# Gate and up projection of a decoder layer: tokens as the stationary operand, 512 features moving, result transposed by VectorE blocks and DMA

## Chip, core and metric

One core of a Trainium2 chip runs the whole layer in one launch. The metric is the device time in microseconds (us), median of three runs. TensorE multiplies a stationary operand (128 x 128, loaded by a weight load of its own) with a moving operand of up to 512 columns and adds into PSUM banks of 128 x 512 fp32. VectorE (DVE), ScalarE (ACT) and GpSimd (POOL) do the elementwise work; SyncE (SP) issues the DMAs. Each engine works through its own queue in order.

## The reference, cut to what matters

One decoder layer on 256 tokens, model width 2048, in fp32. Attention comes first; the part that the change touches is the feed-forward block at the end, with 5632 hidden features:

```python
x = x + jnp.concatenate([o_mla, o_nsa], axis=-1) @ w_o[l]
h = rmsnorm(x, ffn_norm_g[l])
x = x + (jax.nn.silu(h @ w_gate[l]) * (h @ w_up[l])) @ w_down[l]
return rmsnorm(x, final_norm_g)
```

## The kernel before, in words

**Precision.** Every product is made of three: each fp32 operand is split into a high part `hi` (rounded to the fp32r format that TensorE takes) and the rest `lo`, and hi·hi, hi·lo and lo·hi are added in PSUM. For a weight tile ACT writes `whi` (the copy in L142) and DVE writes `wlo` (the subtraction in L144).

**The weight stream.** All weights pass as 354 tiles of 128 x 1024 (512 KB each; the first 16 are 880 wide) through one class, `Stream`. Tile n is loaded by a DMA on SP into one of three raw buffers (`wraw`, L118 to L121), split into one of three pairs (`whi`, `wlo`), and used by TensorE. A raw buffer comes free when the split of the tile three places earlier has been read out; a pair comes free when TensorE is done with the tile three places earlier. `get` (L150) records, in front of each use of tile n, the DMAs up to tile n+2 and the splits up to tile n+1.

**The order.** `program()` (L34) writes TensorE's order by hand. The queues of the other engines, SP's among them, are ordered by a scheduler from the recorded program; a DMA that waits on SP holds up every DMA behind it.

**The feed-forward block.** The normalised input, transposed, lies in `h2T` as 16 blocks of 128 model features by 256 tokens, high and low part side by side (512 columns); `transpose_x` (L650) writes it. The factor of the row norm (`rstd`) is put on later. For gate and up (`gate_up`, L789) the weights are stationary: a tile holds 8 blocks of 128 x 128 weights for one group of 128 hidden features. For each block, `whi` is loaded and 512 columns move (all of `h2T`, L798), then `wlo` is loaded and 256 columns move (the high part, L801). The result comes out as features x tokens, which is what `down` needs. `activate` (L822) adds the two halves of the bank (ACT and DVE), multiplies by the norm's factor, which was spread over the partitions by two TensorE transposes (`rb2`, L208), on POOL (L831), takes the silu on ACT, multiplies on DVE, and splits into `aT`. There are 44 feature groups, in two halves of 22; after each half comes `down` for that half (88 weight tiles in all), in which `aT` is stationary and the weights move, 512 columns at a time: per tile twelve matmuls of 512 columns (L863 to L865).

Gate and up are 176 weight tiles, numbers 90 to 177 and 222 to 309; down has 178 to 221 and 310 to 353. A tile of either kind has 6144 moving columns.

Of the kernel before, what the change touches and what calls it, by code (L numbers as in the profile page):

```python
# [16 lines left out]
P = 128  # L17
# [1 line left out]
D = 2048  # L19
KD = D // P  # L20
FF = 5632
NF = FF // P
NFH = NF // 2
EPS = 1e-6
NEG = -1e30
C_Q, C_KV, C_KR, C_NQ = 0, 512, 768, 832
# [7 lines left out]
def program():  # L34

    s = [("w", ("g1", k)) for k in range(KD)]

    def w(*keys):
        return [("w", k) for k in keys]

    def A(name, i):
        return [(name, i, 0), (name, i, 1)]

    s += [("rb0",)] + w(("q", 0, 0), ("q", 0, 1)) + [("gates",)] + w(("q", 1, 0)) + [("rope_k",)]
    s += w(("w1k", 0), ("q", 1, 1), ("w1k", 1), ("cq", 0, 0)) + [("ck",)] + w(("cq", 0, 1))
# [34 lines left out]
    for h in range(2):  # L80
        for f in range(h * NFH, (h + 1) * NFH):
            if f == 0:
                s += w(("gate", 0, 0), ("up", 0, 0)) + [("tp", 3)] + w(("gate", 1, 0), ("up", 1, 0))
                s += [("rb2",)] + w(("gate", 0, 1), ("up", 0, 1), ("gate", 1, 1), ("up", 1, 1))
            elif f > 1:
                s += w(*A("gate", f), *A("up", f))
        s += [("w", ("down", h, dg, j)) for dg in range(4) for j in range(NFH // 2)]
    return s


# [69 lines left out]
def layer_kernel(ctx: ExitStack, tc: tile.TileContext, a: dict, out: bass.AP):  # L160
# [489 lines left out]
    def transpose_x(dg):  # L650

        for k2 in range(2):
            tp = bank("S0" if k2 == 0 else "O", f"tp{dg}_{k2}")
            for kk in range(2):
                k = 4 * dg + 2 * k2 + kk
                for t in range(2):
                    nc.tensor.transpose(tp[:, kk * S + t * P:kk * S + (t + 1) * P], x[:, t, k * P:(k + 1) * P], ident)
            for kk in range(2):
                k = 4 * dg + 2 * k2 + kk
                g = gcols[:, 16 + k:17 + k]  # L660
                src = tp[:, kk * S:(kk + 1) * S]
                nc.scalar.activation(h2T[:, k, 0, :], src, AF.Copy, scale=g)
                nc.vector.scalar_tensor_tensor(h2T[:, k, 1, :], src, g, h2T[:, k, 0, :].bitcast(F32),
                                               op0=ALU.mult, op1=ALU.subtract)


    def w_in_block(key, w):
# [118 lines left out]
             "mpv": mla_pv, "tp": transpose_x}[op](*args)  # L786


    def gate_up(key, w):  # L789
        n, f, j = key  # L790
        hi, lo = w
        if j == 0:
            st[n, f] = bank("ds" if n == "gate" else "PT", f"{n}{f}")
        pt = st[n, f]
        for k2 in range(0, 8, 2):
            for kk in (k2, k2 + 1):
                k = 8 * j + kk
# [6 lines left out]
    while step[0] == "w":  # L804
        gate_up(step[1], W.get(step[1]))
        step = next(steps)
    transpose_x(*step[1:])
    nc.vector.tensor_reduce(ssq[:, 1, :, 0], ssq[:, 0, :, 0:4], axis=AX.X, op=ALU.add)
    rms_rstd(rstd[:, 3, :], ssq[:, 1, :, 0], D)
    att.close()  # L810

    fp = ctx.enter_context(tc.tile_pool(name="ffn", bufs=1))
    aT = fp.tile([P, NFH, 2, S], F32R, name="aT")
    gfin = fp.tile([P, D], F32, name="gfin")
    nc.gpsimd.dma_start(gfin, a["gfin"])
    W.apart = {len(order) - 2: fp, len(order) - 1: fp}

    def next_weights(*key):
        assert next(steps) == ("w", key)
        return W.get(key)  # L820

    def activate(h, f):  # L822

        t2 = fp.tile([P, 2, S], F32, tag="t2", name=f"t2_{h}_{f}", bufs=2)
        u = fp.tile([P, 2, S], F32, tag="gu", name=f"u_{h}_{f}", bufs=2)
        sl = fp.tile([P, S], F32, tag="sl", name=f"sl_{h}_{f}", bufs=2)
        for b, n in enumerate(("gate", "up")):
            pt = st[n, h * NFH + f]
            nc.scalar.copy(t2[:, b, :], pt[:, S:])
            nc.vector.tensor_add(t2[:, b, :], pt[:, 0:S], t2[:, b, :])  # L830
        nc.gpsimd.tensor_mul(u, t2, RB[:, None, :].to_broadcast([P, 2, S]))  # L831
        nc.scalar.activation(sl, u[:, 0, :], AF.Silu)
        nc.vector.tensor_mul(u[:, 1, :], sl, u[:, 1, :])
        split(aT[:, f, 0, :], aT[:, f, 1, :], u[:, 1, :])

    for h in range(2):
        done = 0
        while done < NFH:
            step = next(steps)
            if step[0] == "rb2":  # L840
                bcast_rows(RB, rstd[:, 3, :], bank2("ps_rb2")[:, 0, :])
                continue
            n, f, j = step[1]
            gate_up(step[1], W.get(step[1]))
            if (n, j) == ("up", 1):
                activate(h, f - h * NFH)
                done += 1
        for dg in range(4):
            if dg % 2 == 0:
                dn = bank2(f"dn{h}_{dg}")  # L850
                pts = [dn[:, 0, :], dn[:, 1, :]]
            else:
                pts = [bank("S0", f"dn{h}_{dg}_0"), bank("O", f"dn{h}_{dg}_1")]
            last = h == 1 and dg == 3
            ntile = NFH // 2

            def down(t, j, w, pt, first, end, c=slice(0, 512)):
                hi, lo = w
                for k in range(2):
                    f = 2 * j + k  # L860
                    wh, wl = (v[:, k * 512 + c.start:k * 512 + c.stop] for v in (hi, lo))
                    h_, l_ = aT[:, f, 0, t * P:(t + 1) * P], aT[:, f, 1, t * P:(t + 1) * P]
                    nc.tensor.matmul(pt, h_, wh, start=f == 2 * first, stop=False)  # L863
                    nc.tensor.matmul(pt, h_, wl, start=False, stop=False)  # L864
                    nc.tensor.matmul(pt, l_, wh, start=False, stop=f == 2 * end - 1)  # L865

            def add(t, c0, c1, pt, i):
# [69 lines left out]
def _pack(inp):  # L937
# [11 lines left out]
    for i, k in enumerate(order):  # L949
# [105 lines left out]
```

## Time and profile before

| | |
|---|---|
| Time, median of three runs (lowest, highest) | 1074.83 us (1074.31, 1075.9) |
| The profiled execution: its time, its span | 1075.57 us, 1073.8 us |
| TensorE busy | 1052.7 us, 98% of the span |
| VectorE, ScalarE, GpSimd busy | 652.9, 565.8, 207.5 us |
| Granted TensorE clock, mean | 0.994 of full speed |
| Weights: DMAs of 512 KB, DMA engines' share | 338, 53.6% |

The span counts from the first to the last instruction. A busy share of TensorE counts overlapping matmuls once, so it tells that the engine seldom waits, not how fast its columns pass; that is read from the starts of matmuls that follow each other. "L142" is line 142 of the kernel; `whi`, `wlo`, `wraw`, `aT`, `h2T` are the names of the buffers, `dn` is the result of `down`, `gate` and `up` those of the two projections.

### The profile page before, as it was taken

To read this page: it belongs to the slowest core of one execution; us is meant where nothing else is said; L and a number is where in the kernel's file an instruction comes from. 1 tells how busy PE (TensorE), PEld (TensorE's weight loads), DVE (VectorE), ACT (ScalarE), POOL (GpSimd) and SP (SyncE) were. 2 spreads that over 40 slices of the span, in tenths; PEclk is the share of its full clock that TensorE was granted. 3 is DMA by queue.
4 is the path that set the end of the run, shared out by engine and by line. 5 is a ranking of instruction groups with operands and counts; after the bars stand their busy time and mean duration, and the time that the engine had idled before them with its cause. 6 is when DMAs were issued, how large, how long until landed. Compare 5 with 4: busy or idle time off the path is not lost.

```text
span 1073.8 us, 16240 instructions
## 1 busy us (share of the span) xinstructions
PE 1052.7 (98%) x6126; PEld 923.7 (86%) x6126; DVE 652.9 (61%) x1004; ACT 565.8 (53%) x996; POOL 207.5 (19%) x209
## 2 busy tenths in 40 slices
PE   8999999899999999999999999999999999999997
PEld 8999999788888888888888888888888888888886
DVE  5678989875656555555555454455555555555554
ACT  5768888754455545545444333345454454444442
POOL 2244446433342101001010000001010010101110
PEclk9999999999999999999999999999999999999998
DMA  8854343334456555555555555555555555555553
GB/s 278 281 168 159 119 133 105 99 105 151 136 178 216 182 192 193 183 193 187 188 194 185 193 193 194 196 194 183 192 189 186 194 184 189 195 186 190 195 194 137
DMA packets 54831, 193.57 MB, mean 180 GB/s; under 512 B 6436, under 2 KB 7076, under 8 KB 54624
## 3 DMA queue, kind: packets, MB, share of 16 engines
q1 hardware_dynamic: 54288, 191.36, 53.6%
q0 software_dynamic: 464, 1.17, 0.3%
q8 instruction: 48, 0.79, 0.3%
q14 instruction: 31, 0.25, 0.1%
HBM read 190.41 MB, written 2.10 MB: 179 GB/s over the span
## 4 chain that ended last, share of the span: by engine, by line
PE 90%; DVE 3%; DMA 3%; ACT 1%; POOL 1%; issue 1%; SPq 0%; POOLq 0%; DVEq 0%; ACTq 0%
PE up L798 15%; PE gate L798 15%; PE gate L801 8%; PE up L801 8%; PE dn L863 7%; PE dn L864 7%; PE dn L865 7%; PE woM L743 1%; PE woM L744 1%; PE woM L745 1%; PE woN L745 1%; PE woN L743 1%; PE woN L744 1%; PE ps_q L213 1%; PE ps_q L214 1%; PE ps_q L215 1%
## 5 line engine op out<-in xcount | busy, mean ns | idle before, releaser
L144 DVE TENSOR_TENSOR wlo<-wraw,whi 128x1024 fp32r<-128x1024 f32 (+3 forms) x352 | 421.1, 1197 | 376.1 <-ACT whi L142 374.8
L142 ACT CAST whi<-wraw 128x1024 fp32r<-128x1024 f32 (+2 forms) x352 | 366.4, 1041 | 438.7 <-PE dn L865 126.7
L798 PE MATMUL gate<-h2T,whi 128*128 128x512 f32 x704 | 221.2, 396 | 0.0
L798 PE MATMUL up<-h2T,whi 128*128 128x512 f32 x704 | 221.1, 395 | 0.0
L831 POOL TENSOR_TENSOR u<-t,RB 128x512 f32<-128x512 f32 x44 | 57.1, 1298 | 554.0 <-DVE t L830 554.0
L801 PEld LDWEIGHTS up<-h2T,wlo 128*128 128x128 f32 x704 | 132.3, 188 | 31.3
L801 PEld LDWEIGHTS gate<-h2T,wlo 128*128 128x128 f32 x704 | 132.2, 188 | 31.2
L801 PE MATMUL gate<-h2T,wlo 128*128 128x256 f32 x704 | 138.3, 278 | 0.0
L801 PE MATMUL up<-h2T,wlo 128*128 128x256 f32 x704 | 138.3, 278 | 0.0
L863 PE MATMUL dn<-whi,aT 128*128 128x512 f32 x344 | 133.8, 389 | 0.0
L864 PE MATMUL dn<-wlo,aT 128*128 128x512 f32 x344 | 133.8, 389 | 0.0
L865 PE MATMUL dn<-whi,aT 128*128 128x512 f32 x344 | 133.8, 389 | 0.0
L146 POOL TENSOR_TENSOR wlo<-wraw,whi 128x256 fp32r<-128x256 f32 x70 | 88.7, 1267 | 127.0 <-ACT whi L142 113.4
L798 PEld LDWEIGHTS gate<-h2T,whi 128*128 128x128 f32 x704 | 107.3, 189 | 0.2
L798 PEld LDWEIGHTS up<-h2T,whi 128*128 128x128 f32 x704 | 107.2, 189 | 0.0
L865 PEld LDWEIGHTS dn<-whi,aT 128*128 128x128 f32 x344 | 64.6, 188 | 13.5
L863 PEld LDWEIGHTS dn<-whi,aT 128*128 128x128 f32 x344 | 64.6, 188 | 13.4
L864 PEld LDWEIGHTS dn<-wlo,aT 128*128 128x128 f32 x344 | 64.6, 188 | 13.1
L213 PE MATMUL ps_q<-hT,whi 128*128 128x256 f32 x128 | 37.5, 293 | 0.5 <-ACT RB L209 0.5
L214 PE MATMUL ps_q<-hT,whi 128*128 128x256 f32 x128 | 36.2, 283 | 0.0
L215 PE MATMUL ps_q<-hT,wlo 128*128 128x256 f32 x128 | 36.2, 283 | 0.0
L743 PE MATMUL woN<-whi,oT 128*128 128x512 f32 x64 | 26.6, 415 | 0.0
(335 smaller groups left out, 1517.7 us busy)
## 6 DMA issues: line engine op xcount, KB each, us to landing
wraw<-in_w_dram SPq DMA_DIRECT2D x338, 512.0 KB, 3.4
wraw<-in_g_dram SPq DMA_DIRECT2D x14, 440.0 KB, 5.3
x<-in_x_dram SPq DMA_DIRECT2D x4, 512.0 KB, 7.0
xt<-in_xT_dram SPq DMA_DIRECT2D x3, 512.0 KB, 6.0
out_dram<-x SPq DMA_DIRECT2D x5, 256.0 KB, 2.5
gfin<-in_gfin_dram POOLq DMA_DIRECT2D x1, 1024.0 KB, 6.0
out_dram<-x SPq DMA_DIRECT2D x2, 320.0 KB, 2.7
wraw<-in_g_dram SPq DMA_DIRECT2D x2, 256.0 KB, 4.2
```

What stands on the lines that cost most here:

```text
L142: nc.scalar.copy(hi[:, c0:c1], raw[:, c0:c1])
L144: nc.vector.tensor_sub(lo[:, c0:c2], raw[:, c0:c2], hi[:, c0:c2].bitcast(F32))
L146: nc.gpsimd.tensor_sub(lo[:, c2:c1], raw[:, c2:c1], hi[:, c2:c1].bitcast(F32))
L213: nc.tensor.matmul(ps, hi, act[:, 0, :], start=start, stop=False)
L214: nc.tensor.matmul(ps, hi, act[:, 1, :], start=False, stop=False)
L743: nc.tensor.matmul(pts[t], h_, wh, start=first, stop=False)
L798: nc.tensor.matmul(pt, hi[:, kk * P:(kk + 1) * P], h2T[:, k], start=k == 0, stop=False)
L801: nc.tensor.matmul(pt[:, 0:S], lo[:, kk * P:(kk + 1) * P], h2T[:, k, 0, :], start=False, stop=k == KD - 1)
L831: nc.gpsimd.tensor_mul(u, t2, RB[:, None, :].to_broadcast([P, 2, S]))
L863: nc.tensor.matmul(pt, h_, wh, start=f == 2 * first, stop=False)
L864: nc.tensor.matmul(pt, h_, wl, start=False, stop=False)
L865: nc.tensor.matmul(pt, l_, wh, start=False, stop=f == 2 * end - 1)
```

## The change

Gate and up take the form that `down` has. The 5632 features are cut in 11 blocks of 512, in three parts of 4, 4 and 3 blocks, each part followed by `down` for its features. A weight tile now holds 2 blocks of 128 model features by 512 hidden features. For each of these and each half of the tokens, three matmuls of 512 columns run with tokens stationary: hi·whi, hi·wlo, lo·whi. So the result comes out as tokens x features and has to be turned before `down`:

- `silu(b)`: ACT takes the silu from PSUM, with the norm's factor as a scale per partition (`r2`, brought into place by four small DMAs on SP in place of the two TensorE transposes).
- `act(b)`: for each half of the tokens DVE multiplies up, factor and silu out of PSUM and transposes 128 x 512 in blocks of 32 x 32 into `tr`. So that the halves interleave, `h2T` holds even tokens first, then odd ones.
- `move(b)`: 16 DMAs on SP, each from one group of 32 partitions to another (32 partitions x 4 runs of 64 fp32, 32 KB), put the 32 x 32 blocks in place in `ar`; ACT and DVE split `ar` into `aT`.

In TensorE's order `move(b)` stands behind the third tile of the next block's gate, or behind the second tile of `down` for the last block of a part. The copy in L142 and the subtraction in L144 are L144 and L146 of the changed kernel.

```diff
+PARTS = (0, 4), (4, 8), (8, 11)
...
+    for n, (b0, b1) in enumerate(PARTS):
+        moved = []
+        for b in range(b0, b1):
+            i = 2 if b == 0 else 3
+            s += w(*[("gate", b, j) for j in range(i)]) + ([("tp", 3)] if b == 0 else moved)
+            s += w(*[("gate", b, j) for j in range(i, 8)]) + [("silu", b)]
+            s += w(*[("up", b, j) for j in range(8)]) + [("act", b)]
+            moved = [("move", b)]
+        down = w(*[("down", n, dg, j) for dg in range(4) for j in range(2 * (b1 - b0))])
+        s += down[:2] + moved + down[2:]
...
-                src = tp[:, kk * S:(kk + 1) * S]
-                nc.scalar.activation(h2T[:, k, 0, :], src, AF.Copy, scale=g)
...
+                src = tp[:, kk * S:(kk + 1) * S].rearrange("p (c t) -> p t c", t=2)
+                hi, lo = (h2T[:, k, s, :].rearrange("p (t c) -> p t c", t=2) for s in range(2))
+                nc.scalar.activation(hi, src, AF.Copy, scale=g)
+                nc.vector.scalar_tensor_tensor(lo, src, g, hi.bitcast(F32), op0=ALU.mult, op1=ALU.subtract)
...
-                nc.tensor.matmul(pt, hi[:, kk * P:(kk + 1) * P], h2T[:, k], start=k == 0, stop=False)
...
-                nc.tensor.matmul(pt[:, 0:S], lo[:, kk * P:(kk + 1) * P], h2T[:, k, 0, :], start=False, stop=k == KD - 1)
+        for k in range(2):
+            kd = 2 * j + k
+            wh, wl = hi[:, k * 512:(k + 1) * 512], lo[:, k * 512:(k + 1) * 512]
+            for t, pt in enumerate(st[n, b]):
+                h_, l_ = h2T[:, kd, 0, t * P:(t + 1) * P], h2T[:, kd, 1, t * P:(t + 1) * P]
+                nc.tensor.matmul(pt, h_, wh, start=kd == 0, stop=False)
+                nc.tensor.matmul(pt, h_, wl, start=False, stop=False)
+                nc.tensor.matmul(pt, l_, wh, start=False, stop=kd == KD - 1)
...
+            nc.sync.dma_start(r2[64 * t:64 * t + 64, m:m + 1], rstd[m::2, 3, t:t + 1])
...
+    def silu(b):
+        for t in range(2):
+            sl = fp.tile([P, 512], F32, tag="sl", name=f"sl{b}_{t}", bufs=2)
+            nc.scalar.activation(sl, st["gate", b][t], AF.Silu, scale=r2[:, t:t + 1])
+            st["sl", b, t] = sl
+    def act(b):
+        tr = fp.tile([P, 16, 32, 2], F32, tag="tr", name=f"tr{b}")
+        for t in range(2):
+            av = fp.tile([P, 512], F32, tag="av", name=f"av{b}_{t}", bufs=2)
+            nc.vector.scalar_tensor_tensor(av, st["up", b][t], r2[:, t:t + 1], st["sl", b, t],
+                                           op0=ALU.mult, op1=ALU.mult)
+            nc.vector.transpose(tr[:, :, :, t], av)
+        st["tr", b] = tr
+    def move(b):
+        ar = fp.tile([P, 4, 4, 64], F32, tag="ar", name=f"ar{b}")
+        tr = st["tr", b].rearrange("p (jc jq) c t -> p jc jq (c t)", jq=4)
+        for i in range(4):
+            for jq in range(4):
+                nc.sync.dma_start(ar[32 * jq:32 * jq + 32, :, i, :], tr[32 * i:32 * i + 32, :, jq, :])
+        b0 = [b0 for b0, b1 in PARTS if b0 <= b < b1][0]
+        aT = fp.tile([P, 4, 2, S], F32R, tag=f"aT{b - b0}", name=f"aT{b}")
+        v = ar.rearrange("p j i c -> p j (i c)")
+        split(aT[:, :, 0, :], aT[:, :, 1, :], v)
+        st["aT", b] = aT
```

How the change moves instructions, at three places. First TensorE, in the middle of a gate tile; `gate_0` and `gate_1` of the changed kernel are the banks of the two token halves. Before:

```order
L798 MATMUL gate_4624<-h2T,whi_4586 128x512 x2
L801 MATMUL gate_4624<-h2T,wlo_4587 128x256 x2
L798 MATMUL gate_4624<-h2T,whi_4620 128x512 x2
L801 MATMUL gate_4624<-h2T,wlo_4621 128x256 x2
L798 MATMUL gate_4624<-h2T,whi_4620 128x512 x2
```

Now:

```order
L810 MATMUL gate_0_4519<-whi_4490,h2T 128x512
L811 MATMUL gate_0_4519<-wlo_4491,h2T 128x512
L812 MATMUL gate_0_4519<-whi_4490,h2T 128x512
L810 MATMUL gate_1_4520<-whi_4490,h2T 128x512
L811 MATMUL gate_1_4520<-wlo_4491,h2T 128x512
L812 MATMUL gate_1_4520<-whi_4490,h2T 128x512
```

Two matmuls of 512 and two of 256 columns with four weight loads became three of 512 with three.

Second SP, where the first block is moved; tiles 106 to 113 are the second block's gate, and `ar0` is the moved first block. Before, tiles 110 to 114 follow each other:

```order
L121 DMA wraw110_4663<-in_w_dram 128x1024
L121 DMA wraw111_4686<-in_w_dram 128x1024
L121 DMA wraw112_4720<-in_w_dram 128x1024
L121 DMA wraw113_4743<-in_w_dram 128x1024
L121 DMA wraw114_4765<-in_w_dram 128x1024
```

Now:

```order
L123 DMA wraw110_4551<-in_w_dram 128x1024
L123 DMA wraw111_4589<-in_w_dram 128x1024
L865 DMA ar0_4569<-tr0_4506 32x4x64 x16
L123 DMA wraw112_4607<-in_w_dram 128x1024
L123 DMA wraw113_4625<-in_w_dram 128x1024
```

The sixteen moves stand between the weight tiles that are the sixth and the seventh of the next block; so it is at all eleven moves.

Third DVE, at the end of the first block's up (tile 105) and in the tiles behind it:

```order
L146 TENSOR_TENSOR wlo107_4516<-wraw107_4488,whi107_4515 128x1024
L854 SCALAR_TENSOR_TENSOR av0_0_4507<-up0_0_4366,r2_4237,sl0_0_4356 128x512
L854 SCALAR_TENSOR_TENSOR av0_1_4510<-up0_1_4367,r2_4237,sl0_1_4358 128x512
L856 STREAM_TRANSPOSE tr0_4506<-av0_0_4507 128x512
L146 TENSOR_TENSOR wlo108_4536<-wraw108_4513,whi108_4535 128x1024
L856 STREAM_TRANSPOSE tr0_4506<-av0_1_4510 128x512
L146 TENSOR_TENSOR wlo109_4554<-wraw109_4533,whi109_4553 128x1024
L146 TENSOR_TENSOR wlo110_4592<-wraw110_4551,whi110_4591 128x1024
L146 TENSOR_TENSOR wlo111_4610<-wraw111_4589,whi111_4609 128x1024
L550 TENSOR_TENSOR aT0_4586<-ar0_4569,aT0_4586 128x4x256
L146 TENSOR_TENSOR wlo112_4628<-wraw112_4607,whi112_4627 128x1024
```

Before, DVE had at each feature group four operations of 128 x 256 between the `wlo` of four tiles; now four of 128 x 512 stand together at the end of a block, with one `wlo` among them, and the split of the moved block stands in front of the seventh tile's. ACT's queue has the copy into `aT0` at the same place, between `whi111` and `whi112`.

## Rows read from the trace of the kernel before

**Rows 1.** The page: busy time by engine, and the last chain's shares.

```profile
PE 1052.7 (98%) x6126; PEld 923.7 (86%) x6126; DVE 652.9 (61%) x1004; ACT 565.8 (53%) x996; POOL 207.5 (19%) x209
PE 90%; DVE 3%; DMA 3%; ACT 1%; POOL 1%; issue 1%; SPq 0%; POOLq 0%; DVEq 0%; ACTq 0%
```

**Rows 2.** Timeline of TensorE: start, length in us, engine, line, operation.

```profile
346.58 0.71 PE L798 MATMUL gate<-h2T,whi 128*128 128x512 f32 x2
...
399.62 0.63 PE L798 MATMUL up<-h2T,whi 128*128 128x512 f32 x2
400.08 0.40 PE L801 MATMUL up<-h2T,wlo 128*128 128x256 f32 x2
400.32 0.63 PE L798 MATMUL up<-h2T,whi 128*128 128x512 f32 x2
...
580.75 0.40 PE L863 MATMUL dn<-whi,aT 128*128 128x512 f32 x1
580.99 0.39 PE L864 MATMUL dn<-wlo,aT 128*128 128x512 f32 x1
```

**Rows 3.** Timeline of VectorE, where two results of down are added (22 tiles apart).

```profile
610.88 1.28 DVE L870 TENSOR_TENSOR x<-x,dn 128x512 f32<-128x512 f32 x2 [0.41 <-PE dn L865]
...
670.72 1.29 DVE L870 TENSOR_TENSOR x<-x,dn 128x512 f32<-128x512 f32 x2 [0.41 <-PE dn L865]
```

**Rows 4.** Timeline of all engines, one weight tile in down; idle before, and releaser.

```profile
599.80 0.39 PE L863 MATMUL dn<-whi,aT 128*128 128x512 f32 x1
600.00 1.05 ACT L142 CAST whi<-wraw 128x1024 fp32r<-128x1024 f32 x1 [1.67 <-PE dn L865]
...
601.09 1.23 DVE L144 TENSOR_TENSOR wlo<-wraw,whi 128x1024 fp32r<-128x1024 f32 x1 [1.50 <-ACT whi L142]
...
602.34 0.33 SPq L121 DMA_DIRECT2D wraw<-in_w_dram  x1
```

**Rows 5.** Weight buffers in 590 to 640 us: from issue to landing.

```profile
DMA to landing us min/median/max: 3.3/3.4/3.5
```

**Rows 6.** The page's DMA issues: queue, count, KB each, us from issue to landing.

```profile
out_dram<-x SPq DMA_DIRECT2D x5, 256.0 KB, 2.5
...
gcols<-in_gcols_dram SPq DMA_DIRECT2D x1, 19.0 KB, 1.8
```

**Rows 7.** Timeline of SP's queue at the start: DMAs issued one behind the other.

```profile
1.17 0.42 SPq L267 DMA_DIRECT2D xt<-in_xT_dram  x1
1.64 0.90 SPq L121 DMA_DIRECT2D wraw<-in_g_dram  x2
2.58 0.44 SPq L269 DMA_DIRECT2D xt<-in_xT_dram  x1
```

**Rows 8.** Issues of output DMAs (SP) and of one on POOL: nanoseconds, min/median/max.

```profile
L887 SPq DMA_DIRECT2D out_dram<-x x8: 332/400/458, 1063.1 to 1069.7; - x8
...
L815 POOL DMA_DIRECT2D gfin<-in_gfin_dram x1: 652/652/652, 337.3 to 337.3; - x1
```

**Rows 9.** VectorE's addition out of PSUM, 128 x 512: nanoseconds, min/median/max.

```profile
L870 DVE TENSOR_TENSOR x<-x,dn x15: 680/681/689, 610.9 to 1060.1; 128x512 f32<-128x512 f32 x15
```

**Rows 10.** Waits of TensorE: us in total, times, longest.

```profile
PE o L512 <- DVE pl L498: 2.6, 1, 2.6
PE ps_ropeq L590 <- DVE u_uq L595: 2.4, 1, 2.4
PE ps_hk L400 <- DVE hsk L395: 1.3, 1, 1.3
```

**Rows 11.** Stretches around these: us, busy PE PEld DVE ACT POOL, PEclk, DMA, GB/s.

```profile
189.00:192.00 3.00, 0.96 (x3) 0.87 (x4) 2.93 (x8) 3.00 (x9) 1.40 (x3) 0.83 0.56 175
192.00:195.00 3.00, 3.00 (x17) 2.82 (x16) 2.39 (x5) 2.52 (x8) 1.44 (x1) 0.60 0.08 14
213.00:216.00 3.00, 1.97 (x7) 1.41 (x8) 2.52 (x4) 1.24 (x2) 0.73 (x2) 0.82 0.01 3
216.00:219.00 3.00, 3.00 (x18) 3.00 (x18) 2.54 (x4) 0.00 (x0) 0.65 (x1) 0.61 0.46 172
```

More of the change, by code (lines that the diff above doesn't have):

```diff
@@ L21 @@
 FF = 5632
-NF = FF // P
-NFH = NF // 2
+PARTS = (0, 4), (4, 8), (8, 11)
 EPS = 1e-6
@@ L79, in program @@
         s += w(("woM", dg, 0), ("woM", dg, 1)) + [("tp", dg - 1)] + w(("woM", dg, 2), ("woM", dg, 3))
[L80 to L87, printed above, removed]
+    for n, (b0, b1) in enumerate(PARTS):
[8 more added lines that the diff above has]
+        s += down[:2] + moved + down[2:]
     return s
@@ L660, in transpose_x @@
                 g = gcols[:, 16 + k:17 + k]
-                src = tp[:, kk * S:(kk + 1) * S]
-                nc.scalar.activation(h2T[:, k, 0, :], src, AF.Copy, scale=g)
-                nc.vector.scalar_tensor_tensor(h2T[:, k, 1, :], src, g, h2T[:, k, 0, :].bitcast(F32),
-                                               op0=ALU.mult, op1=ALU.subtract)
+                src = tp[:, kk * S:(kk + 1) * S].rearrange("p (c t) -> p t c", t=2)
+                hi, lo = (h2T[:, k, s, :].rearrange("p (t c) -> p t c", t=2) for s in range(2))
+                nc.scalar.activation(hi, src, AF.Copy, scale=g)
+                nc.vector.scalar_tensor_tensor(lo, src, g, hi.bitcast(F32), op0=ALU.mult, op1=ALU.subtract)
     def w_in_block(key, w):
@@ L786, in layer_kernel, with pair @@
              "mpv": mla_pv, "tp": transpose_x}[op](*args)
+    def pair(n, name):
+        if n == "S1":
+            b = bank2(name)
+            return [b[:, 0, :], b[:, 1, :]]
+        return [bank(t, f"{name}_{i}") for i, t in enumerate(("S0", "O") if n == "S0" else (n, n))]
     def gate_up(key, w):
-        n, f, j = key
+        n, b, j = key
         hi, lo = w
         if j == 0:
[L793 to L797, printed above, removed]
-                nc.tensor.matmul(pt, hi[:, kk * P:(kk + 1) * P], h2T[:, k], start=k == 0, stop=False)
-            for kk in (k2, k2 + 1):
-                k = 8 * j + kk
-                nc.tensor.matmul(pt[:, 0:S], lo[:, kk * P:(kk + 1) * P], h2T[:, k, 0, :], start=False, stop=k == KD - 1)
-    W.share = 0
-    while step[0] == "w":
-        gate_up(step[1], W.get(step[1]))
+            i = b - [b0 for b0, b1 in PARTS if b0 <= b < b1][0]
+            st[n, b] = pair((("ds", "PT") if i % 2 == 0 else ("S0", "S1"))[n == "up"], f"{n}{b}")
+        for k in range(2):
[6 more added lines that the diff above has]
+                nc.tensor.matmul(pt, l_, wh, start=False, stop=kd == KD - 1)
+    W.share = 0
+    while True:
+        if step[0] == "w":
+            gate_up(step[1], W.get(step[1]))
+        else:
+            transpose_x(*step[1:])
+            break
         step = next(steps)
-    transpose_x(*step[1:])
     nc.vector.tensor_reduce(ssq[:, 1, :, 0], ssq[:, 0, :, 0:4], axis=AX.X, op=ALU.add)
     rms_rstd(rstd[:, 3, :], ssq[:, 1, :, 0], D)
+    r2 = cp.tile([P, 2], F32, name="r2")
+    for t in range(2):
+        for m in range(2):
+            nc.sync.dma_start(r2[64 * t:64 * t + 64, m:m + 1], rstd[m::2, 3, t:t + 1])
     att.close()
     fp = ctx.enter_context(tc.tile_pool(name="ffn", bufs=1))
-    aT = fp.tile([P, NFH, 2, S], F32R, name="aT")
     gfin = fp.tile([P, D], F32, name="gfin")
@@ L818, in next_weights @@
     def next_weights(*key):
[L819 to L834, printed above, removed]
@@ L836, in layer_kernel @@
-    for h in range(2):
+        while True:
+            step = next(steps)
+            if step[0] == "w":
+                assert step[1] == key
+                return W.get(key)
+            other(*step)
+    def silu(b):
[5 more added lines that the diff above has]
+        tr = fp.tile([P, 16, 32, 2], F32, tag="tr", name=f"tr{b}")
+        for t in range(2):
+            av = fp.tile([P, 512], F32, tag="av", name=f"av{b}_{t}", bufs=2)
[3 more added lines that the diff above has]
+        st["tr", b] = tr
@@ L837, in layer_kernel, with other @@
+    def other(op, *args):
+        {"silu": silu, "act": act, "move": move}[op](*args)
+    for h, (b0, b1) in enumerate(PARTS):
+        ntile = 2 * (b1 - b0)
         done = 0
-        while done < NFH:
+        while done < b1 - b0:
             step = next(steps)
[L840 to L847, printed above, removed]
@@ L848, in layer_kernel @@
-        for dg in range(4):
[L849 to L855, printed above, removed]
+            if step[0] == "w":
+                gate_up(step[1], W.get(step[1]))
+            else:
+                other(*step)
+                done += step[0] == "act"
+        last_part = h == len(PARTS) - 1
@@ L857, in down @@
+        kinds = ("ds", "PT", "S0", "S1") if (b1 - b0) % 2 == 0 else ("S0", "S1", "ds", "S0")
+        for dg in range(4):
+            pts = pair(kinds[dg], f"dn{h}_{dg}")
+            last = last_part and dg == 3
             def down(t, j, w, pt, first, end, c=slice(0, 512)):
@@ L861, in down @@
                     wh, wl = (v[:, k * 512 + c.start:k * 512 + c.stop] for v in (hi, lo))
-                    h_, l_ = aT[:, f, 0, t * P:(t + 1) * P], aT[:, f, 1, t * P:(t + 1) * P]
+                    aT = st["aT", b0 + f // 4]
+                    h_, l_ = aT[:, f % 4, 0, t * P:(t + 1) * P], aT[:, f % 4, 1, t * P:(t + 1) * P]
                     nc.tensor.matmul(pt, h_, wh, start=f == 2 * first, stop=False)
@@ L870, in add @@
                 nc.vector.tensor_add(xs, xs, pt)
-                if h == 1:
+                if last_part:
                     sq = fp.tile([P, 512], F32, tag="sq", name=f"fsq{t}{c0}", bufs=2)
@@ L905, in layer_kernel @@
                     add(t, cs, cs + 512, pts[t], dg)
-                    if h == 1:
+                    if last_part:
                         weigh(t, cs, cs + 512)
@@ L966, in _pack @@
         elif n in ("gate", "up"):
-            w[i] = _chunks(inp["w_" + n][0], 8 * k[2], 8 * k[2] + 8, k[1] * P, (k[1] + 1) * P)
+            w[i] = _chunks(inp["w_" + n][0], 2 * k[2], 2 * k[2] + 2, 512 * k[1], 512 * k[1] + 512)
         elif n == "down":
-            r = k[1] * NFH + 2 * k[3]
+            r = 4 * PARTS[k[1]][0] + 2 * k[3]
             w[i] = _chunks(inp["w_down"][0], r, r + 2, 512 * k[2], 512 * k[2] + 512)
```

## The prediction

> **What bounds the kernel now.** I read the page first: TensorE is busy 98% of the span and holds 90% of the chain that ended last [rows 1], so a change is worth what it does to the rate of TensorE's columns and what it lets TensorE wait. The rate comes from starts of matmuls in the timeline. In gate and up a pair of 512-column and a pair of 256-column matmuls take from 399.62 to 400.32, 0.70 us. Over the 84 tiles from 94 (346.58) to the first of down (580.75) that is 234.17 us, 2.788 a tile [rows 2]. In down two additions that are 22 tiles apart start 59.84 us apart, 2.720 a tile [rows 3]. Both kinds have 6144 columns, so gate and up lose 0.068 us a tile.
>
> The second thing to read is the weight chain, since the change puts 16 DMAs into the one queue that feeds it. Take the tile that TensorE begins at 599.80: the cast of the next but one starts 0.20 later (1.05), its subtraction at 601.09 (1.23), and when that has ended, SP issues at 602.34 the load into the buffer that came free, 2.54 us into the tile [rows 4]. The load lands 3.4 us after its issue [rows 5]. From issue to the first matmul on `wlo` it is 3.4 + 1.05 + 1.23 and some 0.2 between them, 5.9 us; the `whi` is there 1.3 sooner. I count from E, the end of a block's up. The tile behind the moves is the seventh of the next block: due at E + 16.32, its `wlo` two matmuls later, E + 16.55. So it must be issued by E + 10.65; without moves it would be at about E + 5.2. **SP's slack is 5.4 us.**
>
> **The change, part by part.**
>
> *The form of gate and up.* Three matmuls of 512 columns take the place of two of 512 and two of 256, exactly down's form, with the same columns in a tile. I take down's period for it: 176 x 0.068 = 11.9 us saved [rows 2, 3]. The two TensorE transposes for the norm's factor go: some 0.15 more. **-12.1.** The four small DMAs that replace them stand four tiles ahead of what they hold up, far from the first silu, and cost nothing.
>
> *The elementwise work.* The two silus a block stand on ACT and the adds, POOL's multiplications and the many small splits go: ACT and DVE were busy 53% and 61% [rows 1] and get less to do. At a block's end DVE has two products out of PSUM, two transposes, and one `wlo` among them. A product is priced by the addition out of PSUM of the same shape, 0.68 [rows 9]; it has one operand more, which I give nothing. No row shows a VectorE transpose: it lies between 0.3, half of the addition, and 1.23, the subtraction of twice its size [rows 4, 9]; I take half the latter, 0.62, as it is an operation between buffers like that one. The `wlo` of the tile before ends at E - 0.2, so: products to E + 1.2, a transpose to 1.8, `wlo` to 3.1, second transpose to 3.7. The delay of that `wlo` is under 2 us and the tile for it is due two tiles on: covered. The first move is issued at E + 3.75.
>
> For a 128x128 transpose of 16-bit values the Trainium skill (VectorE: DVE Perf Modes, The three transpose paths) states 311 ns; an estimate from that page, four times as much for four times the columns, is 1.24 us. By it the moves would begin 1.2 us later and the sum would be some 13.6 us higher. No run here shows it yet.
>
> *The moves.* Sixteen to a block, on SP, each 32 KB in 128 runs of 256 B. Each issue holds SP for a spacing m, and behind them waits the load of the seventh tile, with all later loads, then the cast on ACT, the subtraction on DVE, and TensorE. That load is issued at E + 3.75 + 16m and used from E + 9.65 + 16m; due is E + 16.55. **The stall is 16m - 6.9 us a block, none below m = 0.43.** So m decides all. Bounds: a weight load is 0.33 [rows 4], with the 0.05 between two issues 0.38. Loads issued one behind the other at the start are spaced 0.47 (1.17 to 1.64; the next 0.94 for two) [rows 7], output issues are 0.33 to 0.46 [rows 8]. All of these are loads and stores whose descriptors the built program carries ready-made; the moves, like the one DMA issued on POOL, are not of that kind there. POOL's took 652 ns to issue [rows 8], with the gap 0.70. It is another engine and another queue, so it is a bound and not a price. I take the middle of 0.47 and 0.70, **m = 0.58**: a stall of 2.4 us, at ten blocks **24 us**. Some of the later moves also wait for the landing of the eighth before; with eight spacings (4.6 us) against landings of 1.8 to 2.5 [rows 6] that adds nothing.
>
> *The last move.* In parts one and two, of four blocks each, the older three feed down's first six tiles, so the block just finished is needed at the seventh, E + 16.32, which the stall above already covers. In part three, of three blocks, it is needed at down's fifth tile, E + 10.88. There the last move is issued at 3.75 + 15m, lands about 2.0 later [rows 6], and is cast in 1.05 [rows 4], with some 0.8 until the low part follows: the stall is 15m - 3.3, **5.4 us**.
>
> *The clock.* Waits of TensorE of 2.6 and 2.4 us [rows 10] were followed by granted clocks of 0.83 and 0.60, and 0.82 and 0.61, in two stretches of 3 us [rows 11]: 3 x (0.17 + 0.40) = 1.7 us lost each, part of it at the lower of the two levels, 1.2 of 2.4 GHz. My stall of 2.4 is as long, but it is cut in two by one matmul between the wait for `whi` and that for `wlo`. The wait of 1.3 us [rows 10] has no such stretch of its own in the rows. I take the loss for half of ten blocks and for the last: 5 x 1.7 + 1.7 = **10.2**; both ends, 1.7 and 18.7, stay in the range.
>
> *Sum.* -12.1 + 24 + 5.4 + 10.2 = +27.5 on the profiled 1075.57 is 1103.1; the profiled execution lies 0.7 above the median, so **1102 us**.
>
> **The rivals.**
>
> *Faster: issues as short as any on SP in this trace.* With m from 0.38 to 0.46 the load behind the moves is in time or 0.5 us late; what remains is the last block (2.4 to 3.6), one loss of clock and up to 5 us of stalls: -12.1 + 4.1 to -12.1 + 10.5, **1067 to 1073**. For it: every SP issue of before [rows 4, 7, 8]. Against it: none of them is of the moves' kind. The Trainium skill has a sentence for this side (DMA: Bandwidth & Descriptors, Issuing engines are not separate DMA queues): issue time on an engine "is usually small relative to the DMA itself". In this trace 0.33 stands against a landing of 3.4, which agrees for a load of 512 KB; sixteen of 32 KB the rows don't show. Chance 0.18.
>
> *Same: hold and gain cancel.* With m from 0.46 to 0.49 the stalls take 5 to 9 us, the last block 3.6 to 4.1 and one or two losses of clock 2 to 3: 1073 to 1077. Chance 0.10.
>
> *Slower still: the transposes or the moves are late too.* With transposes of 1.23 and m = 0.58, the first move is 1.2 later, the stall 3.6 at ten blocks and 6.6 at the last; with the clock of more blocks lost: about **1118**; with m = 0.70 at the short transposes, 43 + 7.2 + 18.7 - 12.1 = +57, **1132**. Part of slower.
>
> *The form doesn't give down's rate.* Gate and up would stay at 2.788, 12 us above every case: 1114 at my m, and slower even at m = 0.43. Against it: the same sequence of matmuls runs at 2.720 in down for 88 tiles, with the same buffers. Chance 0.03.
>
> **How the numbers follow.** 0.2% (2.1 us) is about what a measurement of this kernel can tell from no change. The forecast, stalls at ten blocks (m over 0.49, the later rivals with it), has 0.72: slower. Same 0.10, faster 0.18. Faster's own low end with m = 0.38 is 1067, the high end with m = 0.70 is 1132; beyond them I leave about 0.1 above (late transposes and slow issues together) and 0.05 below. Since faster and same hold 0.28, the range reaches to them. The slower case's own range is 1080 to 1132.
>
> **What would show it.** In the trace of the changed kernel: the matmul starts in the middle of gate, 2.72 a tile (else the form's term is wrong); SP's issues of `ar<-tr` and their spacing, which is m; the transpose's duration; the waits of TensorE on the cast and the subtraction of the seventh tile of each block, ten times 16m - 6.9, and none in other tiles; a longer wait on `aT` at the last part's fifth tile; the granted clock behind each. I am wrong on the sign if m is 0.46 or less, or if the loads behind the moves turn out to land much faster or slower than 3.4 us, since the moves' short runs share the DMA engines with them.

## The result, and the profile after

The changed kernel took 1137.66 us (median; 1134.05 to 1138.46) against 1075.01 for the kernel before: a ratio of 1.0576, 95% interval 1.0551 to 1.0600. Slower by 62.65 us, where 1102 was predicted; above the range's upper end of 1132. The profiled execution took 1134.05 us, the lowest of the four, with a span of 1132.3 against 1073.8.

The page of the changed kernel, the lines that answer to [rows 1]: busy time, and the shares of the last chain. SP's queue, which had none of the chain, now has 10%, most of it on the line of the moves (L865).

```profile
PE 1071.2 (95%) x5420; PEld 906.4 (80%) x5420; DVE 633.9 (56%) x891; ACT 535.3 (47%) x852; POOL 148.9 (13%) x165
PE 71%; SPq 10%; DVE 8%; DMA 5%; ACT 3%; issue 3%; POOL 0%; POOLq 0%; DVEq 0%; ACTq 0%
SPq L865 9%; PE up L812 7%; PE up L810 7%; PE up L811 7%; PE dn L899 5%; PE dn L900 5%; PE dn L898 5%; DMA wraw<-in_w_dram 4%; PE gate L811 4%; PE gate L812 4%; PE gate L810 3%; DVE wlo L146 3%; ACT whi L144 2%; PE woM L745 1%; PE woM L746 1%
```

The waits of TensorE from gate to the end (total us, times, longest). In the kernel before this stretch had none.

```profile
PE gate L810 <- ACT whi L144: 23.4, 8, 3.3
PE dn L898 <- ACT whi L144: 5.7, 2, 3.0
PE gate L811 <- DVE wlo L146: 5.5, 8, 0.8
PE dn L898 <- ACT aT L549: 5.2, 1, 5.2
PE dn L899 <- DVE wlo L146: 1.1, 3, 0.5
```

Eight blocks wait in the next gate and two in down, for the cast and then for the subtraction of the tile behind the moves; the eleventh waits for its own `aT`. That is the place and the number of times that were forecast. The new operations: nanoseconds, min/median/max, of the products, the transposes and the moves' issues.

```profile
L854 DVE SCALAR_TENSOR_TENSOR av<-up,r,sl x22: 740/744/751, 377.2 to 1050.9; 128x512 f32<-128x512 f32 x22
L856 DVE STREAM_TRANSPOSE tr<-av x22: 698/703/707, 378.5 to 1053.3; 128x512 f32<-128x512 f32 x22
L865 SPq DMA_DIRECT2D ar<-tr x176: 593/599/1275, 381.0 to 1063.6; - x176
```

One stall, in the timeline of all engines but TensorE: the end of the second block (E is 427.27).

```profile
427.09 3.87 SPq L123 DMA_DIRECT2D wraw<-in_w_dram  x2
...
430.52 0.70 DVE L856 STREAM_TRANSPOSE tr<-av 128x512 f32<-128x512 f32 x1
431.25 10.27 SPq L865 DMA_DIRECT2D ar<-tr  x16
...
436.71 1.23 DVE L146 TENSOR_TENSOR wlo<-wraw,whi 128x1024 fp32r<-128x1024 f32 x1 [1.50 <-ACT whi L144]
441.62 9.26 SPq L123 DMA_DIRECT2D wraw<-in_w_dram  x6
442.95 1.05 ACT L549 CAST aT<-ar 128x1024 fp32r<-128x1024 f32 x1 [6.27 <-DMA ar<-tr]
444.03 1.23 DVE L550 TENSOR_TENSOR aT<-ar,aT 128x1024 fp32r<-128x1024 f32 x1 [6.09 <-ACT aT L549]
445.69 1.04 ACT L144 CAST whi<-wraw 128x1024 fp32r<-128x1024 f32 x1 [1.69 <-DMA wraw<-in_w_dram]
446.77 3.76 DVE L146 TENSOR_TENSOR wlo<-wraw,whi 128x1024 fp32r<-128x1024 f32 x3 [1.51 <-ACT whi L144]
```

The moves hold SP from 431.25 to the next load's issue at 441.62, 10.37 us or 0.648 for each of sixteen. ACT waits for that load until 445.69. On TensorE:

```profile
443.36 0.39 PE L812 MATMUL gate<-whi,h2T 128*128 128x512 f32 x1
446.79 0.79 PE L810 MATMUL gate<-whi,h2T 128*128 128x512 f32 x1 [3.04 <-ACT whi L144]
448.05 0.79 PE L811 MATMUL gate<-wlo,h2T 128*128 128x512 f32 x1 [0.47 <-DVE wlo L146]
448.64 0.63 PE L812 MATMUL gate<-whi,h2T 128*128 128x512 f32 x1
449.07 0.63 PE L810 MATMUL gate<-whi,h2T 128*128 128x512 f32 x1
...
455.81 0.39 PE L810 MATMUL up<-whi,h2T 128*128 128x512 f32 x1
...
461.25 0.39 PE L810 MATMUL up<-whi,h2T 128*128 128x512 f32 x1
```

From start to start, 443.36 to 448.05 is 4.69 us for two matmuls that else take 0.45: a stall of 4.2. Behind it a matmul takes 0.43 instead of 0.227 for some four us. The last two rows are two tiles apart, 5.44 us: 2.72 a tile, the rate of down. In stretches of that stall (us, busy PE, PEld, DVE, ACT, POOL, then the granted clock, the DMA engines' share, GB/s):

```profile
443.00:447.00 4.00, 0.96 (x5) 0.50 (x3) 1.46 (x2) 2.08 (x3) 0.00 (x0) 0.92 0.97 345
447.00:451.50 4.50, 4.03 (x9) 2.85 (x10) 3.44 (x3) 2.05 (x2) 0.00 (x0) 0.50 0.65 173
451.50:455.50 4.00, 4.00 (x15) 3.18 (x15) 1.23 (x1) 1.21 (x2) 0.00 (x0) 0.78 0.61 236
```

**The ledger.** From gate's first matmul to down's last it was 731.4 us before and is 791.4 now, 60.0 more. I summed every interval between the starts of neighbouring matmuls there, less the usual 0.227, wherever it was over 0.3. Intervals with a wait in them come to 41.0 us at the ten blocks (3.8 to 4.5 each) and 5.8 at the last (5.4 of it the wait for `aT`); intervals without one, in the time behind a stall, to 24.1 us (1.4 to 3.0 at each of eleven, 2.2 on average); small ones elsewhere to 0.5. 60.0 - 41.0 - 5.8 - 24.1 - 0.5 = -11.4 is the form's gain.

### The profile page after: what moved, and what is told of

It is laid out like the page before. It is cut to its first block, busy times and chain, and to the rows that moved or that the text cites. A ratio compares the mean times of both kernels' runs of the same rounds, so it can differ in the third digit from the quotient of the medians.

```text
span 1132.3 us, 14758 instructions
## 1 busy us (share of the span) xinstructions
PE 1071.2 (95%) x5420; PEld 906.4 (80%) x5420; DVE 633.9 (56%) x891; ACT 535.3 (47%) x852; POOL 148.9 (13%) x165
## 4 chain that ended last, share of the span: by engine, by line
PE 71%; SPq 10%; DVE 8%; DMA 5%; ACT 3%; issue 3%; POOL 0%; POOLq 0%; DVEq 0%; ACTq 0%
SPq L865 9%; PE up L812 7%; PE up L810 7%; PE up L811 7%; PE dn L899 5%; PE dn L900 5%; PE dn L898 5%; DMA wraw<-in_w_dram 4%; PE gate L811 4%; PE gate L812 4%; PE gate L810 3%; DVE wlo L146 3%; ACT whi L144 2%; PE woM L745 1%; PE woM L746 1%
## 5 line engine op out<-in xcount | busy, mean ns | idle before, releaser
L146 DVE TENSOR_TENSOR wlo<-wraw,whi 128x1024 fp32r<-128x1024 f32 (+3 forms) x352 | 416.2, 1183 | 385.1 <-ACT whi L144 382.8
L144 ACT CAST whi<-wraw 128x1024 fp32r<-128x1024 f32 (+2 forms) x352 | 366.4, 1041 | 459.3 <-PE up L812 140.0
L810 PE MATMUL gate<-whi,h2T 128*128 128x512 f32 x352 | 144.2, 410 | 23.4 <-ACT whi L144 23.4
L811 PE MATMUL gate<-wlo,h2T 128*128 128x512 f32 x352 | 145.2, 412 | 5.5 <-DVE wlo L146 5.5
L898 PE MATMUL dn<-whi,aT 128*128 128x512 f32 x344 | 137.2, 399 | 10.9 <-ACT whi L144 5.7
L812 PE MATMUL gate<-whi,h2T 128*128 128x512 f32 x352 | 143.6, 408 | 0.0
L810 PE MATMUL up<-whi,h2T 128*128 128x512 f32 x352 | 136.9, 389 | 0.0
L811 PE MATMUL up<-wlo,h2T 128*128 128x512 f32 x352 | 136.9, 389 | 0.0
L812 PE MATMUL up<-whi,h2T 128*128 128x512 f32 x352 | 136.9, 389 | 0.0
L900 PE MATMUL dn<-whi,aT 128*128 128x512 f32 x344 | 136.5, 397 | 0.0
L926 POOL TENSOR_TENSOR x<-x,gfin 128x512 f32<-128x512 f32 (+1 forms) x7 | 9.7, 1405 | 768.5 <-ACT fsq L908 768.5
L810 PEld LDWEIGHTS gate<-whi,h2T 128*128 128x128 f32 x352 | 70.4, 200 | 41.8 <-ACT whi L144 26.7
L811 PEld LDWEIGHTS gate<-wlo,h2T 128*128 128x128 f32 x352 | 70.1, 199 | 23.3 <-DVE wlo L146 8.4
L812 PEld LDWEIGHTS gate<-whi,h2T 128*128 128x128 f32 x352 | 70.3, 200 | 14.9
L812 PEld LDWEIGHTS up<-whi,h2T 128*128 128x128 f32 x352 | 66.1, 188 | 13.8
L811 PEld LDWEIGHTS up<-wlo,h2T 128*128 128x128 f32 x352 | 66.1, 188 | 13.7
L810 PEld LDWEIGHTS up<-whi,h2T 128*128 128x128 f32 x352 | 66.1, 188 | 13.6
```

What stands on the lines that cost most here:

```text
L144: nc.scalar.copy(hi[:, c0:c1], raw[:, c0:c1])
L146: nc.vector.tensor_sub(lo[:, c0:c2], raw[:, c0:c2], hi[:, c0:c2].bitcast(F32))
L810: nc.tensor.matmul(pt, h_, wh, start=kd == 0, stop=False)
L812: nc.tensor.matmul(pt, l_, wh, start=False, stop=kd == KD - 1)
```

## The experiments

The theory: the moves' issues hold SP's in-order queue for longer than the weight stream's slack, and each stall is followed by matmuls at the low clock (0.50 in the rows above). Rival A: the moves' short runs take the DMA engines from the weights. Rival B: DVE is late at a block's end. Each run has the changed kernel as its base, unless it names another.

### The moves spread among the weight loads

```diff
-        s += down[:2] + moved + down[2:]
+                for q in range(4):
+                    s += [("move", b - 1, q)] + gate[3 + q:4 + q]
...
-        for i in range(4):
-            for jq in range(4):
-                nc.sync.dma_start(ar[32 * jq:32 * jq + 32, :, i, :], tr[32 * i:32 * i + 32, :, jq, :])
+        for jq in range(4):
+            nc.sync.dma_start(ar[32 * jq:32 * jq + 32, :, q, :], tr[32 * q:32 * q + 32, :, jq, :])
```

> The sixteen moves of each of the first ten blocks stay on SP, but stand in three groups (8, 4 and 4) with one weight load between each two; those of the last block stay together. Theory (each move holds SP's queue for 0.64 us, and sixteen in a row are more than the 6.8 us from the first move to the time at which the next load is due): eight hold it for 5.2 us from E + 3.9 to E + 9.1, before the E + 10.65 at which the load behind them is due, four for 2.6. No stall at ten blocks, no low clock behind them; the stall of the last block (5.3 us, and 2.4 of low clock) stays. 1075 - 12.3 + 7.7 = 1070 us, 1069 to 1073. Rival A (the moves' short runs share the DMA engines with the weights and make those land late): the same bytes move, 1115 or more. Rival B (DVE is late at a block's end): nothing of it is changed, 1125 or more.

Measured: 1081.32 us, ratio 1.0048 (1.0033 to 1.0063). The same 176 moves on the same queue, and 56 us less. SP's queue at the first block, and TensorE's waits from gate on:

```profile
379.72 0.33 SPq L134 DMA_DIRECT2D wraw<-in_w_dram  x1
380.40 5.27 SPq L877 DMA_DIRECT2D ar<-tr  x8
385.78 0.53 SPq L134 DMA_DIRECT2D wraw<-in_w_dram  x1
386.35 2.53 SPq L877 DMA_DIRECT2D ar<-tr  x4
```

```profile
PE dn L912 <- ACT aT L560: 7.5, 3, 5.2
PE dn L914 <- DVE aT L561: 1.3, 2, 0.6
PE up L822 <- DVE wlo L157: 0.8, 2, 0.5
PE dn L913 <- DVE wlo L157: 0.6, 1, 0.6
```

No wait for a `whi` is left. Rivals A and B, which kept all their causes here, are out as the main cause. The 11 us above my 1070 are a miss of its own: three waits on `aT`, not one. At the ends of parts one and two the spread moves (12 and 4 there) bring the newest block later than the seventh tile of down wants it; with the low clock behind them the three cost 14.6 us by the ledger's way of counting (4.1, 2.4, 8.2).

### No moves

```diff
-        ar = fp.tile([P, 4, 4, 64], F32, tag="ar", name=f"ar{b}")
-        tr = st["tr", b].rearrange("p (jc jq) c t -> p jc jq (c t)", jq=4)
-        for i in range(4):
-            for jq in range(4):
-                nc.sync.dma_start(ar[32 * jq:32 * jq + 32, :, i, :], tr[32 * i:32 * i + 32, :, jq, :])
+        ar = st["tr", b].rearrange("p (jc jq) c t -> p jc jq (c t)", jq=4)
```

> No moves: the high and low part of aT are split straight from the transposed blocks, so the 32 x 32 blocks stand at wrong places; everything else is computed. Theory: the form's 12.3 us are left and nothing else, 1062.7 us (1061.5 to 1064), with no waits in gate, up and down. Rival B (DVE's products and transposes at the block's end delay the weights): stalls of 2 us or more at each block stay, 1085 or more. If the form gave nothing, 1075.

Measured: 1063.7 us against 1075.9, ratio 0.9888 (0.9874 to 0.9903). All waits of TensorE from gate on:

```profile
PE dn L895 <- DVE wlo L146: 0.5, 1, 0.5
```

The form with its silus, products, transposes and splits is worth 12 us, as forecast, and costs hardly a wait. Everything above 1064 in the changed kernel is the moves.

### The moves on POOL

```diff
-                nc.sync.dma_start(ar[32 * jq:32 * jq + 32, :, i, :], tr[32 * i:32 * i + 32, :, jq, :])
+                nc.gpsimd.dma_start(ar[32 * jq:32 * jq + 32, :, i, :], tr[32 * i:32 * i + 32, :, jq, :])
```

> The sixteen moves of each block are issued on POOL's queue, which has next to nothing to do there; bytes and runs are the same. Theory (the hold of SP's queue): no stall at ten blocks. POOL's one DMA of before took 0.65 us to issue; at 0.70 each the last block's moves end at E + 3.9 + 10.5, and aT10 comes 3.9 later: a stall of 7.4 us and some 2.4 of low clock there. 1075 - 12.3 + 9.8 = 1072.5 us, 1069 to 1078. Rival A (short runs on the DMA engines): 1115 or more. Rival B (DVE late): 1125 or more.

Measured: 1084.33 us, ratio 1.0083 (1.0063 to 1.0103). The moves' issues on POOL, and all waits of TensorE from gate on:

```profile
L865 POOL DMA_DIRECT2D ar<-tr x176: 548/548/612, 382.6 to 1011.3; - x176
```

```profile
PE dn L898 <- ACT aT L549: 11.6, 3, 7.3
PE dn L900 <- DVE aT L550: 1.3, 2, 0.7
```

The weight stream is not held at any block: 53 us come back with one word changed, bytes and runs the same. The last block's wait is 7.3, as expected; again the ends of parts one and two wait too (2.8 each and the low clock behind), which the expectation left out.

### Moves that carry almost nothing

```diff
-            i = 2 if b == 0 else 3
+            i = 2 if b == 0 else 4
...
-        s += down[:2] + moved + down[2:]
+        s += down[:3] + moved + down[3:]
...
-        ar = fp.tile([P, 4, 4, 64], F32, tag="ar", name=f"ar{b}")
+        ar = st["ar"]
...
-                nc.sync.dma_start(ar[32 * jq:32 * jq + 32, :, i, :], tr[32 * i:32 * i + 32, :, jq, :])
+                nc.sync.dma_start(ar[32 * jq:32 * jq + 32, 0, i, 0:1], tr[32 * i:32 * i + 32, 0, jq, 0:1])
```

In `program()` the moves stand one tile later than in the changed kernel, which on SP's queue brings them to nearly the same place.

> Sixteen moves a block on SP at the same place (two of them ahead of the sixth load), but each carries one value for each of 32 partitions, 128 bytes in all, instead of 32 KB; the rest of the moved tile holds a constant, so the result is not the layer's. Theory (the hold is per DMA issued, whatever it carries: the four small DMAs of r2 took 0.586 us each): spacing 0.62 to 0.65, stalls of 3 to 4 us at ten blocks and about 5 at the last, low clock behind each; 1125 to 1138 us. Rival A (bytes and runs): no stalls, 1062 to 1072.

Measured: 1119.51 us, ratio 1.0402 (1.0370 to 1.0433). The issues (nanoseconds), and the largest waits:

```profile
L868 SPq DMA_DIRECT2D ar<-tr x176: 507/589/597, 381.3 to 1051.2; - x176
```

```profile
PE gate L810 <- ACT whi L144: 12.4, 8, 2.5
PE dn L901 <- ACT whi L144: 6.7, 2, 3.4
PE gate L811 <- DVE wlo L146: 6.2, 9, 0.9
PE dn L901 <- ACT aT L549: 3.0, 1, 3.0
```

A move of 128 bytes takes 0.59 us to issue, one of 32 KB 0.60. Rival A expected at most 1072. The time is 5 us under my lower end: where two moves stand ahead of the sixth load, they read only what the first transpose writes and are issued before the second (428.52, with the second from 429.52), so the hold ends sooner, and these blocks' stalls are 2.4 to 3.7 us. In down, where all sixteen stand together, they stand ahead of the sixth tile's load, which is due a tile (2.7 us) sooner than the seventh's; so the two stalls are 4.5 and 4.6, though the load behind the moves is issued 2 us earlier than in the changed kernel.

### What makes an issue dear

The base here is the kernel without moves.

```diff
+        nc.sync.dma_start(k1, st["tr", b].rearrange("p a c t -> p (a c t)"))
...
+        nc.sync.dma_start(k2, tr[0:32, :, 0, :])
...
+        nc.sync.dma_start(k3, a["w"][b][0:32].rearrange("p (j q c) -> p j q c", q=4, c=64)[:, :, 1, :])
```

> The kernel without moves (its aT split straight from tr, blocks at wrong places), with three single DMAs a block on SP whose data nobody reads: tr to another buffer whole, 128 x 1024 (kw); one piece of a move's shape, 32 x 4 x 64, buffer to buffer on the same partitions (ks); a piece of that shape from the weights in DRAM (kd). Which kind makes an issue cost 0.60 us instead of the 0.33 of a weight load? Theory 1 (a source in a buffer on the chip is what is dear): kw and ks 0.58 to 0.60, kd 0.33 to 0.42. Theory 2 (the cut shape is dear): ks and kd 0.58 to 0.60, kw 0.33. Theory 3 (only the crossing of partitions is dear): all three under 0.45. Time 1064 to 1067 us in each case.

Measured: 1061.26 us in one run. The issues on SP, nanoseconds:

```profile
L864 SPq DMA_DIRECT2D kw<-tr x11: 519/522/532, 379.8 to 989.1; - x11
L866 SPq DMA_DIRECT2D ks<-tr x11: 602/607/649, 380.4 to 989.7; - x11
L868 SPq DMA_DIRECT2D kd<-in_w_dram x11: 560/567/717, 334.5 to 364.0; - x11
```

All three theories fall. A whole tile in one piece, a piece on its own partitions and a piece out of DRAM take 0.52, 0.61 and 0.57: neither the source nor the cut nor the crossing alone makes the price. What the three share with the moves and with the norm factor's four DMAs (0.586), and not with weight loads and outputs (0.33 to 0.46 in [rows 4, 7, 8]), is that the built program does not carry their descriptors ready-made. No trace shows this mark. It fits the median of every kind of DMA on SP in these traces, but not each issue: a weight load right behind a move has the mark and took 0.53. It is a correlation: no run gave one DMA both forms, and why an issue is dear stays open.

### One more raw buffer

```diff
-            t = self.pool.tile([P, 1024], F32, tag="wraw", name=f"wraw{i}", bufs=self.DMA_AHEAD)
+            if self.more and i % 4 == 3:
+                t = self.more.tile([P, 1024], F32, tag="wraw", name=f"wraw{i}")
+            else:
+                t = self.pool.tile([P, 1024], F32, tag="wraw", name=f"wraw{i}", bufs=3)
...
+    W.more, W.DMA_AHEAD = fp, 4
```

> The changed kernel with a fourth raw buffer from the gate of the second block's time on; sixteen moves in a row as in it. They then stand behind the seventh tile, and the load behind them is due 2.7 us later. Theory: the stall of a block falls from 3.9 to some 1.2 us at ten blocks; the last block keeps 5.3 and 2.4 of low clock. If waits of 1.2 us leave the granted clock at full speed (one of 1.3 in the kernel before did), 1075 - 12.3 + 12 + 7.7 = 1083 us; if each is followed by as much low clock as now (2.7), 1109 us. Rival (the load behind the moves is late for its own landing, not its issue): stalls of 3 us or more, 1125 or more.

Measured: 1087.85 us, ratio 1.0125 (1.0101 to 1.0149). With sixteen moves in a row as before, the stalls at the ten blocks are 1.0 to 2.0 us from start to start instead of 3.8 to 4.5: they fall by the 2.7 us by which the deadline moved. It also shows the clock's part. Two of its stalls, the second and the third, in stretches (columns as above):

```profile
443.50:445.50 2.00, 1.16 (x5) 0.42 (x3) 1.31 (x2) 1.65 (x2) 0.00 (x0) 1.00 1.01 365
445.50:447.50 2.00, 2.00 (x9) 1.67 (x10) 1.14 (x1) 1.05 (x1) 0.00 (x0) 1.00 0.84 291
...
488.50:490.50 2.00, 1.00 (x4) 0.26 (x2) 1.06 (x2) 1.57 (x2) 0.00 (x0) 1.00 0.98 340
490.50:492.50 2.00, 1.42 (x4) 1.17 (x5) 1.75 (x2) 1.11 (x2) 0.00 (x0) 0.76 0.92 358
492.50:494.50 2.00, 2.00 (x6) 1.51 (x6) 1.23 (x1) 0.45 (x1) 0.00 (x0) 0.50 0.91 295
```

Behind the stall of 1.3 us the clock stays at full speed; behind the one of 2.0 it falls to half, the lower of its two levels, and costs some 1.7 us more. Of the ten stalls only that one was followed by it, one of 1.95 was not; in the changed kernel all eleven were.

### Both repairs: spread moves or moves on POOL, with down's tiles in another order

```diff
-        down = w(*[("down", n, dg, j) for dg in range(4) for j in range(2 * (b1 - b0))])
+        m = 2 * (b1 - b0 - 1)
+        down = [("down", n, dg, j) for js in (range(m), (m, m + 1)) for dg in (0, 1) for j in js]
+        down = w(*down, *[("down", n, dg, j) for dg in (2, 3) for j in range(2 * (b1 - b0))])
```

For the first of the two the moves are spread at all eleven blocks, for the second they are issued on POOL. The cut leaves out the loop of `down`, which now keeps the banks of two groups open.

> The spread moves (8, 4, 4 with a weight load between) at all eleven blocks, and down's tiles in another order: the first two groups of 512 columns take all older blocks first and the newest block behind that, so that it is due six tiles later in parts of four and four tiles later in the last. Theory (what was left in the spread kernel were waits for the newest aT at the three parts' ends, 14.6 us with the low clock behind them, and 3.4 elsewhere): 1081.3 - 14.6 = 1066.7, and if the short waits on wlo go too 1063.5; 1062 to 1068 us. Rival (the low clock or the moves' traffic take time without a wait that is seen): 1075 or more.

Measured: 1066.78 us against 1074.77, ratio 0.9930 (0.9913 to 0.9946). All waits of TensorE from gate on:

```profile
PE dn L915 <- DVE wlo L156: 0.3, 1, 0.3
```

> The moves on POOL and down's tiles in the same new order. Theory: the waits on aT (11.6 us, 8.4 with what follows) were all that the moves on POOL cost; 1084.3 - 20.0 = 1064.3 us, 1062.5 to 1066.5. Rival (issuing on POOL delays other engines): waits of DVE or TensorE stay, 1070 or more.

Measured: 1069.54 us, ratio 0.9953 (0.9938 to 0.9968). One wait on `aT` is left, at the last block (2.8 us with its low part; 4.9 with the low clock). That was the 5 us between expected and measured.

```profile
1008.77 1.04 ACT L146 CAST whi<-wraw 128x1024 fp32r<-128x1024 f32 x1 [1.66 <-PE dn L905]
1009.72 1.04 ACT L551 CAST aT<-ar 128x1024 fp32r<-128x1024 f32 x1
1010.81 0.50 PE L903 MATMUL dn<-whi,aT 128*128 128x512 f32 x1 [2.08 <-ACT aT L551]
```

The moves are not late here: the last had landed by 1003.4, 16.6 us after E, against 17.4 in the spread version. But the cast into `aT` stands in ACT's queue behind the `whi` cast of 1008.77, which waits for TensorE, and so begins 6.3 us after the landing. Both versions compute the whole layer and beat both kernels, by a margin that is small but clear of the intervals; the spread one keeps 8 of the 12 us.

## Why the prediction was wrong, step by step

The mechanism came as it was described. Two terms of the sum were too small: the stall of a block (16m and the landing behind it) and the loss to the clock.

- **What bounds the kernel, and the slack of SP**: right. The stalls are where the count from [rows 4, 5] put them, at the tile behind the moves, ten times, and once on `aT`.
- **The form**: -12.1 forecast; -11.4 in the ledger, and 12.2 between the medians of the run without moves. Right.
- **The elementwise work**: the products took 0.744 for the 0.68 taken from [rows 9], the transposes 0.703 for 0.62. The first move still starts 3.7 us behind E on average (E + 4.0 at five blocks, as in the stall shown, and E + 3.5 at six) for the 3.75 forecast, so this cost the sum nothing. The estimate from the Trainium skill (VectorE: DVE Perf Modes, The three transpose paths), 1.24, is not borne out here: this transpose of 128 x 512 fp32 took 0.703 us.
- **The moves' spacing m**, the term named as deciding all: 0.58 forecast; the usual spacing is 0.644, inside the bounds of 0.38 and 0.70. At some blocks single issues take longer, so that from the first move to the next load 10.35 to 11.1 us pass, 10.6 on average for the 9.3 forecast: 1.3 us a block. The middle of 0.47 and 0.70 was taken although the built program put the moves in the class of the upper one.
- **The landing behind the moves**: 3.4 us was taken from single loads [rows 5]. Behind the moves three buffers are free, so three loads go out within 1.1 us; in the stall shown the first landed 4.0 us after its issue, with the DMA engines at a share of 0.97 in that stretch, and at the ten blocks 3.8 on average. That is 0.4 us a block that the sum did not have. Whether the three slow each other is not shown: with four buffers, where four go out together, the first landed after 3.4 to 3.8. Together: 4.1 us a stall for 2.4, **41.0 us for 24**.
- **The last block**: 5.4 forecast, 5.8 measured, 5.4 of it the wait for the high part of `aT`. That is luck in part: the spacing put 1.0 us more on fifteen moves, the first move was 0.3 earlier, and the 0.8 allowed for the low part was hardly needed as a wait.
- **The clock**: the step that failed most, for its size. Half of ten blocks were to be followed by the loss of 1.7 us read from [rows 10, 11], since one matmul cuts each wait in two; all were, with 2.2 us on average: **24.1 us for 10.2**. At 2.4 us of stall the half would have been a fair guess (of five stalls of 1.95 to 2.4 us in these runs three were followed by it). At 4.1 the matmul in the middle saved nothing. The upper end, 18.7, was too low as well: it had 1.7 for each of the eleven, and they cost 1.4 to 3.0. Why they differ no run shows.
- **Sum**: 17.0 + 0.4 + 13.9 us too little and 0.7 too much gain, 32 of the 35.7 us by which the median missed; the rest is about the 3.6 that lie between the profiled execution and the median of the four, and no trace shows it.
- **The rivals**: short issues (faster) needed m of 0.46 or less. The Trainium skill's sentence behind it (DMA: Bandwidth & Descriptors, Issuing engines are not separate DMA queues), that issue time is usually small beside the DMA, does not hold for this kernel: a move lands 1.9 us after its issue, sixteen issues take 10.4, and moving them to another queue gave back 53 us. "Slower still" was the nearest case, at 1138 where 1132 was given: it had stalls of 4.3 us by m = 0.70, and 4.1 came with a smaller m and a later landing; its loss to the clock was too small.

## What to carry to other kernels

Count a DMA as queue time on the engine that issues it, whatever it carries, and hold the sum of a burst against the slack of what is queued behind it: here sixteen small ones held up a stream that has five microseconds to spare. Splitting the burst into shorter pieces brought the change from 6% slower to 0.5% slower, and with down's tiles in another order to 0.7% faster. A stall of TensorE is to be priced with the slow matmuls behind it, which here cost half as much again as the stall. And when one wait goes, look for the next in line before writing down the gain: the newest `aT` was hidden behind a longer stall in the profile, and with the moves on POOL one cast came late because of its place in ACT's queue.

## What was not expected of the hardware

- A buffer-to-buffer copy of 128 x 1024 in one piece takes 0.522 us of SP's queue, a weight load of the same size 0.33. A weight load issued right behind moves took 0.53.
- A move issued on POOL took 0.548 us, less than on SP (0.599), though the POOL DMA from which the upper bound of m was read had taken 0.652 [rows 8]. It was not the only one there: ten others of the kernel before took 0.52 to 0.73.
- In the stall shown the granted clock began to fall while TensorE still waited (0.92 on average from 443 to 447), was at half until 451.5, and was back within the next four microseconds, though matmuls had flowed since 448.05.
